# An encoder trunk on one core: gate products of the first 256 columns between transposes, the gate's bias added by TensorE, low parts on GpSimd

## The chip, the cores and the metric

The kernel runs on one core of a Trainium2 chip. The metric is the device time of one execution in microseconds. The engines are called by the profile's names: PE (TensorE, with PEld for its weight loads), DVE (VectorE), ACT (ScalarE), POOL (GpSimd) and SP (SyncE, which here only issues DMAs). Each executes its own list of instructions in order and waits on semaphores where it needs another's result.

## The reference

Two encoder layers over 1024 tokens of 1024 features, all in float32. The change concerns what follows the mixer in each layer:

```python
x = layer_norm(DEEPNORM_ALPHA * x + mix @ w_o[i], ln1_g[i], ln1_b[i])
ffn = expert_choice_moe(x, router_w[i], w1[i], w3[i], w2[i])
ple = jax.nn.sigmoid(x @ ple_gate_w[i] + ple_gate_b[i]) * (p[i] @ ple_w[i])
x = layer_norm(DEEPNORM_ALPHA * x + ffn + ple, ln2_g[i], ln2_b[i])
```

The router is a softmax of `x @ router_w` over 16 experts; each expert takes the 128 tokens with the highest affinity. `p` has 256 features per token. "PLE" below is the third line, and its gate is the sigmoid's argument.

## The kernel before, in words

**Precision.** PE multiplies in a reduced form of float32. A float32 operand is therefore split into a high part, which ACT makes by a cast (L82), and a low part, source minus high, made by DVE or POOL (L83). `mm3` (L87 to L89) forms a product by three matmuls: high by high, high by low, low by high.

**The tokens.** They stand in eight tiles of 128. `tail` multiplies the mixer's output by w_o tile by tile (PSUM tiles named S, two buffers) and `residual` makes the layer norm; its result x1 goes to DRAM (`keep_x1`, L1129 and L1132) and stays in SBUF. The last tile's norm is woven into the stage after it.

**The stage of the transposes** (`route`, from `residual(T - 1)`). `turn(t)` transposes tile t of x1 on PE (L157, eight transposes into two PSUM buffers of four) and splits the result: tiles 0 to 3 into xp, 4 to 7 into xk. `p_tile(i)` does the same for a tile of p (L1178, two transposes). The PSUM buffers named ps rotate among four, so that a transpose waits until DVE has taken the low part out of the buffer used four before. The order on PE is: turns 0 to 4, p tiles 0 to 3, the gate's bias by feature (L1215, for the experts' part), turns 5 to 7, p tiles 4 to 7. The order of all engines but SP is the order in which the code is written; SP's is set by a scheduler.

**The router.** Products with rws for 256, 256 and 512 tokens, each copied out by ACT (L1237); eight small transposes (L1241), then a softmax on DVE and ACT (L1244 to L1249, with the exponential on ACT). `back()` (L1258) turns the affinities for the choice of tokens. Between the router's copies ACT already casts PLE weights.

**The PLE's steps.** Tokens 0 to 511 are done here, the other half among the experts. There are sixteen steps: four groups n of 256 columns by four token tiles t. A step has 24 products of the gate (8 feature chunks by three matmuls) into pg and 6 of p @ ple_w into pw, both halves of one ps buffer. DVE adds the bias row (L1339), ACT takes the sigmoid (L1331) and copies pw (L1332, one buffer wv), POOL multiplies (L1333) and after two tiles issues a DMA that adds the result to acc in DRAM (L1335). `Feed` splits the weights ahead: of each ten, POOL takes six low parts and DVE four; sixteen split tiles (wk) rotate. Into the steps are woven: `back()` in step 0, sixteen rounds of top-k on DVE (L1267 to L1270), `merged` and `chosen` in the last steps. Raw weights lie in two rings; the first four gate chunks of 1 MB come through `ring_slot`.

**The experts** follow: about 1200 us of both layers together with PE multiplying, while 1 MB loads run ahead.

Of the kernel before, what the change touches and what calls it, by code (L numbers as in the profile page):

```python
# [20 lines left out]
D = 1024  # L21
S = 1024
T = 8
KC = 8
EPS = 1e-6
ALPHA = 4.0 ** 0.25
NEXP = 16
# [3 lines left out]
class Feed:  # L31
# [34 lines left out]
    def get(self, i):  # L66
        self.upto(i)
        return self.tiles[i]
# [6 lines left out]
class Body:  # L75
# [1071 lines left out]
    def route(self, L, x1, pl, residual, b, ctx_x):  # L1147

        nc, tc, h = self.nc, self.tc, self.h
        acc_d = self.acc_d[L]  # L1150
        TP = 4
        SP, SK = TP * 128, S - TP * 128
# [15 lines left out]
        rw = a.tile([128, KC, NEXP], F32, name="rw")  # L1168
        nc.sync.dma_start(rw, h["router_w"][L].rearrange("(k p) e -> p k e", p=128))
# [16 lines left out]
        for n in range(D // CW):  # L1186
            chunks.append(([128, KC, CW], [(lambda t: t, wg[:, :, n * CW:(n + 1) * CW])],
                           [lambda t, k=k: t[:, k, :] for k in range(KC)]))
            order += [(n, k) for k in range(KC)] + [(D // CW, 2 * n + k) for k in range(2)]
        chunks.append(([128, 2, D], [(lambda t: t, wp)],  # L1190
                       [lambda t, n=n, k=k: t[:, k, n * CW:(n + 1) * CW] for n in range(D // CW) for k in range(2)]))
        ring2 = lambda shape: raw2.tile(shape, F32, name="raw2", tag="raw2", bufs=5)
        feed = Feed(self, None, chunks, CW, WB, lo=[nc.gpsimd] * 6 + [nc.vector] * 4,
                    rings=[self.ring_slot] * 4 + [ring2], order=order)
        for k in range(4):
            feed.load(k)
# [1 line left out]
        def turn(t):  # L1198
            dst, u = (xp, t) if t < TP else (xk, t - TP)
            self.transpose_split(x1[t], dst[0], dst[1], u)  # L1200

        stats, scale, bias = residual(T - 1)
        turn(0)
        self.weave(stats[:2])
        turn(1)
        self.weave(stats[2:])
        turn(2)
        self.weave(scale)
        turn(3)
        turn(4)  # L1210
        self.weave(bias)
        for i in range(4):
            p_tile(i)
        pb = self.ps((128, KC))
        nc.tensor.transpose(pb, br, self.ident[:KC, :KC])  # L1215
        nc.vector.tensor_copy(bf, pb)
        self.split(rw, rws[:, 0], rws[:, 1])
        turn(5)
        turn(6)
        turn(7)  # L1220
        for i in range(4, T):
            p_tile(i)
        self.dump(f"x1_{L}", self.x1_d[L])
        ctx_x.close()
# [5 lines left out]
        brows = [c.tile([128, CW], F32, name="brow", bufs=2)]  # L1230
# [44 lines left out]

        def merged():

            tf = a.tile([48, 128], F32, name="tf")
            bt = a.tile([16, 2, 128], F32, name="bt")
            mt = a.tile([16, 3, 128], F32, name="mt")  # L1280
# [18 lines left out]
            self.dump(f"idx_{L}", idx)  # L1299

        step = 0
        for n in range(D // CW):
            cs = slice(n * CW, (n + 1) * CW)
            brow = brows.pop() if brows else c.tile([128, CW], F32, name="brow", bufs=2)
            self.row_bcast(brow, h["ple_gate_b"][L][cs])
            for t in range(TP):
                sl = slice(t * 128, (t + 1) * 128)
                if t % 2 == 0:
                    sgp = out2.tile([128, 2, CW], F32, name="sgT", bufs=2)
                sg = sgp[:, t % 2, :]  # L1310
                wv = out2.tile([128, CW], F32, name="wv", bufs=1)
                pgw = self.ps()
                pg, pw = pgw[:, :CW], pgw[:, CW:2 * CW]
                for k in range(10):
                    if t == 0:
                        feed.upto(10 * n + min(k + 1, 9))
                    w = feed.get(10 * n + k)
                    if k < KC:
                        self.mm3(pg, xp[0][:, k, sl], xp[1][:, k, sl], w[:, 0, :], w[:, 1, :], k == 0, k == KC - 1)
                    else:  # L1320
                        self.mm3(pw, pp[:, 0, k - KC, sl], pp[:, 1, k - KC, sl], w[:, 0, :], w[:, 1, :],
                                 k == KC, k == 9)
                    if t == TP - 1:
                        feed.upto(10 * n + min(k, 3) + WB)
# [5 lines left out]
                def finish(sg=sg, wv=wv, pw=pw, t=t, cs=cs, sgp=sgp):  # L1330
                    nc.scalar.activation(sg, sg, AF.Sigmoid)  # L1331
                    nc.scalar.copy(wv, pw)  # L1332
                    nc.gpsimd.tensor_mul(sg, sg, wv)  # L1333
                    if t % 2 == 1:
                        nc.gpsimd.dma_start(acc_d[(t - 1) * 128:(t + 1) * 128, cs].rearrange("(t p) c -> p t c", p=128), sgp,  # L1335
                                            accum_op=OP.add)

                step += 1
                nc.vector.tensor_add(sg, pg, brow)  # L1339
                if step == TP * D // CW:  # L1340
                    break
                if t == 0:
                    feed.upto(10 * n + WB - 1)
                for r in range(16 * (step - 1) // 13, min(16, 16 * step // 13)):
# [57 lines left out]
    def experts(self, L, gates, idx, idxf, count, moe, xk, pk, bf, SP, SK, out2, last):  # L1402
        nc, tc, h = self.nc, self.tc, self.h
        x1_d, acc_d = self.x1_d[L], self.acc_d[L]
        with ExitStack() as ctx:
# [89 lines left out]
            def ple(f):  # L1495

                pg, pw = self.ps(), self.ps()
                for k in range(10):
                    j = at[("ple", f, 0), k // 5]
                    feed.upto(j + LA)  # L1500
                    w = feed.get(j)
                    c = slice((k % 5) * 128, (k % 5) * 128 + 128)
                    if k < KC:
                        self.mm3(pg[:, :SK], w[:, 0, c], w[:, 1, c], xk[0][:, k, :], xk[1][:, k, :], k == 0, k == KC - 1)
                    else:
                        self.mm3(pw[:, :SK], w[:, 0, c], w[:, 1, c], pk[:, 0, k - KC, :], pk[:, 1, k - KC, :],
                                 k == KC, k == 9)
                    feed.drop(j)
                sg = out2.tile([128, SK], F32, name="sgT", bufs=2)
                nc.scalar.activation(sg, pg[:, :SK], AF.Sigmoid, bias=bf[:, f:f + 1])  # L1510
                nc.vector.tensor_mul(sg, sg, pw[:, :SK])

                def out():
                    p = self.ps((128, SK // 128, 128))
                    for t in range(SK // 128):
                        nc.tensor.transpose(p[:, t, :], sg[:, t * 128:(t + 1) * 128], self.ident)
                    ev = out2.tile([128, SK], F32, name="ev", bufs=2).rearrange("p (t c) -> p t c", c=128)
# [414 lines left out]
```

## Time and profile before

| | us |
|---|---|
| median of three runs | 2713.09 (2711.2 to 2713.68) |
| profiled execution, its own time | 2715.39 |
| its span, first to last instruction | 2713.7 |
| PE busy in the span | 2607.9 (96%) |
| DVE, ACT, POOL busy | 2192.4, 1769.1, 780.9 |
| mean granted TensorE clock | 0.982 of full |

A row of the timeline gives the start, the time until the last of the merged instructions ended, engine, line, operation and the number of instructions; in brackets stands the idle time before it and who ended it. A window's row gives each engine's busy time, the granted clock as a share of 2.4 GHz (0.50 is 1.2 GHz) and what the DMA engines did. The two layers go through the stage alike: layer 0 from 624.5 us on, layer 1 from 1967.2 us on.

### The profile page before, as it was taken

What the parts mean: (1) busy time and instruction counts of PE and PEld (TensorE: products, weight loads), DVE (VectorE), ACT (ScalarE), POOL (GpSimd) and SP (SyncE); (2) the same over time, 40 slices, a digit from 0 to 9 for tenths busy, and PEclk for the clock granted to TensorE, in tenths of its full rate; (3) what the DMA queues carried; (4) which work ended last, traced back from release to release, by engine and by line L of the source; (5) the groups of instructions that cost most, each with busy time, mean ns of one, the idle gap of its engine ahead of it and who ended that gap; (6) DMA issues with size and microseconds to landing.
All of it is one profiled execution on the core that took longest, in us unless ns stands there. A gap on an engine that the chain in (4) does not pass through costs nothing.

```text
span 2713.7 us, 37590 instructions
## 1 busy us (share of the span) xinstructions
PE 2607.9 (96%) x13446; PEld 2166.0 (80%) x13446; DVE 2192.4 (81%) x3084; ACT 1769.1 (65%) x2655; POOL 780.9 (29%) x682
## 2 busy tenths in 40 slices
PE   8996899998999999999899999999989999999996
PEld 7886688787988888888677788887878888888884
DVE  3448787765888888988888989997668888888897
ACT  3335688714577777877542799997056777777783
POOL 0023456302401101110363577663143101110104
PEclk9997999999999999999899999999999999999998
DMA  4215200364799999999620010004658999999994
GB/s 171 78 57 151 68 9 11 115 229 151 229 344 367 364 377 385 363 365 370 235 108 16 36 28 13 13 13 117 221 154 271 356 371 365 364 374 369 384 363 162
DMA packets 223178, 579.11 MB, mean 213 GB/s; under 512 B 19360, under 2 KB 87088, under 8 KB 222992
## 3 DMA queue, kind: packets, MB, share of 16 engines
q1 hardware_dynamic: 201264, 535.82, 53.0%
q0 software_dynamic: 21728, 40.90, 7.1%
q8 instruction: 106, 1.74, 0.3%
q14 instruction: 80, 0.66, 0.1%
HBM read 511.52 MB, written 63.96 MB: 212 GB/s over the span
## 4 chain that ended last, share of the span: by engine, by line
PE 84%; DVE 7%; ACT 4%; issue 2%; DMA 1%; POOL 1%; DVEq 0%; POOLq 0%; ACTq 0%; SPq 0%
PE S L87 11%; PE S L89 11%; PE S L88 11%; PE ps L87 9%; PE ps L89 8%; PE ps L88 8%; PE S L660 6%; PE ps L698 6%; PE ps L723 5%; PE ps L157 3%; PE ps L1689 2%; ACT pt L82 1%; PE ps L1691 1%; ACT p L667 1%; DVE st L556 1%
## 5 line engine op out<-in xcount | busy, mean ns | idle before, releaser
L83 DVE TENSOR_TENSOR wm<-raw,wm 128x1024 fp32r<-128x1024 f32 (+1 forms) x798 | 905.1, 1206 | 23.3 <-ACT wm L82 13.7
L82 ACT CAST wm<-raw 128x1024 fp32r<-128x1024 f32 (+1 forms) x800 | 783.2, 1046 | 80.5 <-PE S L89 76.1
L87 PE MATMUL S<-wm,xs 128*128 128x512 f32 x1024 | 401.3, 392 | 0.5 <-ACT xs L82 0.5
L89 PE MATMUL S<-wm,xs 128*128 128x512 f32 x1024 | 398.8, 389 | 0.0
L88 PE MATMUL S<-wm,xs 128*128 128x512 f32 x1024 | 398.5, 389 | 0.0
L689 POOL TENSOR_SCALAR p<-p,mx 128x1024 f32<-128x1024 f32 x190 | 214.5, 1129 | 188.4 <-DVE mx L688 181.1
L663 DVE TENSOR_REDUCE mx<-S 128x1 f32<-128x1024 f32 x192 | 234.3, 1221 | 38.1 <-PE S L660 32.9
L83 DVE TENSOR_TENSOR pt<-ps,pt 128x512 fp32r<-128x512 f32 x384 | 245.2, 680 | 23.6 <-ACT pt L82 22.5
L1492 POOL DMA_INDIRECT acc_d<-y,idx x30 | 48.4, 1615 | 748.6 <-ACT y L1491 648.6
L82 ACT CAST pt<-ps 128x512 fp32r<-128x512 f32 x384 | 206.2, 588 | 35.9 <-PE ps L723 34.7
L89 PEld LDWEIGHTS S<-wm,xs 128*128 128x128 f32 x1024 | 192.2, 188 | 41.0 <-DVE xs L83 0.9
L87 PEld LDWEIGHTS S<-wm,xs 128*128 128x128 f32 x1024 | 192.3, 188 | 39.7 <-ACT xs L82 1.0
L88 PEld LDWEIGHTS S<-wm,xs 128*128 128x128 f32 x1024 | 192.3, 188 | 38.7
L667 ACT ACTIVATE p<-S,mx 128x1024 f32<-128x1024 f32 x190 | 214.0, 1126 | 11.4 <-DVE mx L663 10.6
L723 PE MATMUL ps<-ident,p 128*128 128x128 f32 x1520 | 202.5, 274 | 7.2 <-DVE pt L83 4.6
L723 PEld LDWEIGHTS ps<-ident,p 128*128 128x128 f32 x1520 | 177.8, 141 | 38.1 <-DVE pt L83 6.6
L87 PE MATMUL ps<-wm,hh 128*128 128x512 f32 x480 | 189.6, 395 | 0.0
L89 PE MATMUL ps<-wm,hh 128*128 128x512 f32 x480 | 187.2, 390 | 0.0
L88 PE MATMUL ps<-wm,hh 128*128 128x512 f32 x480 | 186.9, 389 | 0.0
L698 PE MATMUL ps<-pt,vhl 128*128 128x512 f32 x512 | 149.6, 414 | 0.0
L1519 POOL DMA_DIRECT2D acc_d<-ev x16 | 22.3, 1397 | 320.0 <-ACT ev L1518 280.7
L940 ACT ACTIVATE mv<-mv 128x1 f32<-128x1 f32 x32 | 6.5, 203 | 160.1 <-DVE mv L939 160.1
(454 smaller groups left out, 5467.7 us busy)
## 6 DMA issues: line engine op xcount, KB each, us to landing
raw<-in_w_dram SPq DMA_DIRECT2D x384, 1024.0 KB
raw<-in_w_o_dram SPq DMA_DIRECT2D x8, 1024.0 KB
raw<-in_ple_gate_w_dram SPq DMA_DIRECT2D x8, 1024.0 KB
x_d<-x SPq DMA_DIRECT2D x16, 512.0 KB
acc_d<-r SPq DMA_DIRECT2D x16, 512.0 KB
raw<-in_ple_gate_w_dram SPq DMA_DIRECT2D x16, 512.0 KB
r<-acc_d SPq DMA_DIRECT2D x16, 512.0 KB
raw<-in_w_in_even_dram SPq DMA_DIRECT2D x6, 1024.0 KB
```

The costliest lines, as they stand in the source:

```text
L82: self.nc.scalar.copy(hi, src)
L83: (eng or self.nc.vector).tensor_sub(lo, src, hi.bitcast(F32))
L87: mm(out, lh, rh, start=start, stop=False)
L88: mm(out, lh, rl, start=False, stop=False)
L89: mm(out, ll, rh, start=False, stop=stop)
L157: nc.tensor.transpose(p[:, k, :], src[:, (4 * j + k) * 128:(4 * j + k + 1) * 128], self.ident)
L660: nc.tensor.matmul(s[:, n * 512:(n + 1) * 512], u["q"][j][:, u["qt"] * 128:(u["qt"] + 1) * 128], u["k"][j][:, n * 512:(n + 1) * 512], star ...
L663: nc.vector.tensor_reduce(mx[:, 0:1], s, axis=AX.X, op=OP.max, negate=True)
L667: self.nc.scalar.activation(p, u["s"], AF.Exp, bias=mx[:, 0:1], accum_out=mx[:, 1:2])
L689: nc.gpsimd.tensor_scalar(P[i], P[i], mx[:, 2:3], 1.0, op0=OP.mult, op1=OP.mult)
L698: nc.tensor.matmul(po[g], v(4 * half + m), pt[half][z][:, m, :], start=half + m + z == 0, stop=half == 1 and m == 3 and z == 1)
L723: nc.tensor.transpose(pp[:, m, :], p[:, kt * 128:(kt + 1) * 128], self.ident)
```

## The change

Of the gate, the first group of columns (n = 0) for the four tiles t leaves the steps: `early_gate(t)` computes it into an S buffer between the later turns, and ACT puts its sigmoid in sg0. Its eight weight tiles are split in pairs by `early_weights(i)`, with the low parts on POOL, the first pair into wa, the others into the buffers of x1's tiles 0 to 2, which are then no longer needed. In every gate the bias is added by two matmuls: `pick`, a constant that selects row n of four, times the high and low parts of the bias rows, `bros`; the DVE addition goes. All four p tiles of the middle move behind turn 7. The low parts of all PLE weights go to POOL. Top-k rounds are set out by a new table, in which steps 0 to 2 and 4 have none; rw moves to a pool of its own, and two tiles of `merged` and one of the experts' move to other memory.

```diff
-        feed = Feed(self, None, chunks, CW, WB, lo=[nc.gpsimd] * 6 + [nc.vector] * 4,
+        feed = Feed(self, None, chunks, CW, WB, lo=nc.gpsimd,
                     rings=[self.ring_slot] * 4 + [ring2], order=order)
...
+        for n in range(NB):
+            nc.gpsimd.tensor_copy(pick[:, n, :], self.ident[:NB, n:n + 1].to_broadcast([NB, 128]))
...
+        brow = e.tile([NB, CW], F32, name="brow")
+        nc.sync.dma_start(brow, h["ple_gate_b"][L].rearrange("(n c) -> n c", c=CW))
...
+        def early_weights(i):
+            w = wa if i == 0 else b.tile([128, 2, 2, CW], F32R, name=f"x1_{i - 1}")
+            for j in range(2):
+                k = 2 * i + j
+                w0[k] = w[:, j]
+                self.split(feed.raw[0][:, k, :], w[:, j, 0, :], w[:, j, 1, :], nc.gpsimd)
...
+        def gate(pg, t, w, n):
+            sl = slice(t * 128, (t + 1) * 128)
+            for z in range(2):
+                nc.tensor.matmul(pg, pick[:, n, :], bros[:, z, :], start=z == 0, stop=False)
+            for k in range(KC):
+                wk = w(k)
+                self.mm3(pg, xp[0][:, k, sl], xp[1][:, k, sl], wk[:, 0, :], wk[:, 1, :], False, k == KC - 1)
...
+        def early_gate(t):
+            if t % 2 == 0:
+                pgs.append(self.ps2())
+            pg = pgs[-1][:, (t % 2) * 512:(t % 2) * 512 + CW]
+            gate(pg, t, w0.get, 0)
+            nc.scalar.activation(sg0[:, t, :], pg, AF.Sigmoid)
...
         stats, scale, bias = residual(T - 1)
+        self.split(brow, bros[:, 0, :], bros[:, 1, :], nc.gpsimd)
+        early_weights(0)
         turn(0)
         self.weave(stats[:2])
         turn(1)
         self.weave(stats[2:])
+        early_weights(1)
         turn(2)
         self.weave(scale)
+        early_weights(2)
         turn(3)
+        early_weights(3)
         turn(4)
         self.weave(bias)
-        for i in range(4):
-            p_tile(i)
+        early_gate(0)
...
+        turn(5)
+        early_gate(1)
         self.split(rw, rws[:, 0], rws[:, 1])
-        turn(5)
         turn(6)
+        early_gate(2)
         turn(7)
-        for i in range(4, T):
+        early_gate(3)
+        for i in range(T):
             p_tile(i)
...
+        ROUNDS = [0, 0, 0, 1, 1] + [1 + 15 * i // 9 for i in range(1, 10)] + [16] * 3
...
+                if n:
+                    gate(pg, t, get, n)
...
-                    nc.scalar.activation(sg, sg, AF.Sigmoid)
+                    if n:
+                        nc.scalar.activation(sg, pg, AF.Sigmoid)
                     nc.scalar.copy(wv, pw)
-                    nc.gpsimd.tensor_mul(sg, sg, wv)
+                    nc.gpsimd.tensor_mul(sg, sg if n else sg0[:, t, :], wv)
...
-                nc.vector.tensor_add(sg, pg, brow)
```

What the change does to ACT's list at the head of the stage in layer 0 (a difference, + is new; mv is the last tile's norm, L945 its scaling, x_0 to x_2 the reused buffers with weights):

```order
 L940 ACTIVATE mv<-mv 128x1
+L82 CAST bros<-brow 4x256
+L82 CAST wa<-raw 128x256 x2
 L82 CAST xp_5464<-ps 128x4x128 x4
 L940 ACTIVATE mv<-mv 128x1
+L82 CAST x_0_5537<-raw 128x256 x2
 L82 CAST xp_5464<-ps 128x4x128 x2
 L945 ACTIVATE x_7_4805<-r,mv 128x512 x2
+L82 CAST x_1_5563<-raw 128x256 x2
 L82 CAST xp_5464<-ps 128x4x128 x2
+L82 CAST x_2_5582<-raw 128x256 x2
 L82 CAST xk_5450<-ps 128x4x128 x2
```

The casts of the bias rows and of the weights stand ahead of those of the turned tiles.

SP's queue at the same place (the new load of w is one of the experts' chunks, into the ring slot of the first gate chunk):

```order
 L1166 DMA br<-in_ple_gate_b_dram 8x128
-L1169 DMA rw<-in_router_w_dram 128x8x16
+L1212 DMA rw<-in_router_w_dram 128x8x16
+L1215 DMA brow<-in_ple_gate_b_dram 4x256
+L47 DMA raw<-in_w_dram 128x2x1024
 L1129 DMA x_d_76<-x_7_4805 128x1024
 L1132 DMA acc_d_78<-r 128x1024
```

The bias rows, brow, are asked for third, and a 1 MB load has moved ahead of the last tile's stores.

PE's list behind the router in layer 0, as it is now (lg and af are the router's scores and affinities, pp is p turned):

```order
L1288 MATMUL ps<-ident,lg 128x16 x8
L87 MATMUL ps<-wk,pp 128x256
L88 MATMUL ps<-wk,pp 128x256
L89 MATMUL ps<-wk,pp 128x256
L87 MATMUL ps<-wk,pp 128x256
L88 MATMUL ps<-wk,pp 128x256
L89 MATMUL ps<-wk,pp 128x256
L1305 MATMUL ps<-ident,af 16x128 x8
```

Before, 24 products with xp stood between the first row and the second; they are in the transposes' stage now.

## Rows read from the trace of the kernel before

**Rows 1.** The page, the chain that ended last: shares of the span by engine.

```profile
PE 84%; DVE 7%; ACT 4%; issue 2%; DMA 1%; POOL 1%; DVEq 0%; POOLq 0%; ACTq 0%; SPq 0%
```

**Rows 2.** Windows of layer 0: the transposes, the PLE's steps, the experts.

```profile
core 0: us, PE busy (x) PEld busy (x) DVE busy (x) ACT busy (x) POOL busy (x), PEclk, DMA share, GB/s
624.50:646.35 21.85, 14.92 (x83) 11.41 (x81) 16.95 (x36) 12.72 (x27) 3.55 (x3) 0.77 0.34 108
...
658.50:715.00 56.50, 56.50 (x481) 56.17 (x481) 48.02 (x123) 25.08 (x69) 33.24 (x42) 1.00 0.52 131
...
740.00:800.00 60.00, 60.00 (x283) 49.77 (x282) 51.82 (x50) 45.10 (x52) 5.84 (x4) 1.00 0.95 334
```

**Rows 3.** The timeline of PE in the transposes of layer 0.

```profile
624.49 1.91 PE L157 MATMUL ps<-ident,x 128*128 128x128 f32 x16
...
635.65 2.48 PE L1178 MATMUL ps<-ident,pl 128*128 128x128 f32 x8 [2.99 <-DVE xp L83]
...
639.31 5.30 PE L157 MATMUL ps<-ident,x 128*128 128x128 f32 x24
...
646.35 0.29 PE L87 MATMUL ps<-xp,rws 128*16 128x256 f32 x1
```

**Rows 4.** The timeline of ACT in the same stretch.

```profile
625.12 2.06 ACT L82 CAST xp<-ps 128x512 fp32r<-128x512 f32 x4 [8.04 <-PE ps L157]
...
632.89 1.52 ACT L945 ACTIVATE x<-r,mv 128x512 f32<-128x512 f32 x2 [1.77 <-DVE mv L969]
634.31 1.05 ACT L82 CAST xp<-ps 128x512 fp32r<-128x512 f32 x2
```

**Rows 5.** The timeline of SP's queue in the same stretch.

```profile
624.68 0.34 SPq L1166 DMA_DIRECT2D br<-in_ple_gate_b_dram  x1
625.12 0.40 SPq L1169 DMA_DIRECT2D rw<-in_router_w_dram  x1
```

**Rows 6.** Windows of half a microsecond behind the issue of rw.

```profile
626.00:626.50 0.50, 0.40 (x4) 0.16 (x2) 0.50 (x2) 0.50 (x2) 0.00 (x0) 1.00 0.41 47
626.50:627.00 0.50, 0.37 (x3) 0.37 (x4) 0.50 (x2) 0.50 (x2) 0.00 (x0) 1.00 0.87 84
627.00:627.50 0.50, 0.50 (x5) 0.32 (x4) 0.50 (x2) 0.18 (x1) 0.00 (x0) 1.00 0.00 0
```

**Rows 7.** Timelines of SP, ACT and PE in the transposes of layer 1.

```profile
1964.72 0.43 SPq L1169 DMA_DIRECT2D rw<-in_router_w_dram  x1
...
1967.79 2.05 ACT L82 CAST xp<-ps 128x512 fp32r<-128x512 f32 x4 [8.04 <-PE ps L157]
...
1976.97 1.05 ACT L82 CAST xp<-ps 128x512 fp32r<-128x512 f32 x2
...
1988.58 0.29 PE L87 MATMUL ps<-xp,rws 128*16 128x256 f32 x1
```

**Rows 8.** Timelines of DVE, ACT and POOL around the router of layer 0.

```profile
645.88 1.44 DVE L83 TENSOR_TENSOR pk<-ps,pk 128x256 fp32r<-128x256 f32 x4
...
649.56 1.32 ACT L82 CAST wk<-raw 128x256 fp32r<-128x256 f32 x4
...
650.04 4.41 POOL L83 TENSOR_TENSOR wk<-raw,wk 128x256 fp32r<-128x256 f32 x6 [10.31 <-ACT wk L82]
```

**Rows 9.** Timelines of ACT and DVE behind the router of layer 0.

```profile
660.38 0.31 ACT L1246 ACTIVATE af<-af 128x128 f32<-128x128 f32 x1
...
661.28 0.29 DVE L1249 TENSOR_TENSOR af<-af,sm 128x128 f32<-128x128 f32 x1
...
662.91 1.18 ACT L1259 COPY aff<-ps 16x512 f32<-16x512 f32 x2 [2.21 <-PE ps L1258]
```

**Rows 10.** The timeline of POOL in the PLE's steps of layer 0.

```profile
676.85 1.21 POOL L1335 DMA_DIRECT2D acc_d<-sgT  x1 [0.31 <-POOL sgT L1333]
677.65 4.63 POOL L83 TENSOR_TENSOR wk<-raw,wk 128x256 fp32r<-128x256 f32 x6
```

**Rows 11.** Windows of the transposes of layer 0, cut where the granted clock changes.

```profile
626.00:634.00 8.00, 4.16 (x28) 2.67 (x26) 5.87 (x15) 3.46 (x8) 0.22 (x1) 1.00 0.08 9
634.00:644.50 10.50, 7.93 (x34) 6.52 (x35) 8.05 (x17) 6.95 (x15) 3.33 (x3) 0.51 0.49 167
```

**Rows 12.** Groups of instructions in the PLE's steps of layer 0.

```profile
L1333 POOL TENSOR_TENSOR sgT<-sgT,wv 128x256 f32<-128x256 f32 x14 | 11.6, 832 | 14.7 <-ACT wv L1332 14.7
L1267 DVE MAX8 top<-aff 48x8 f32<-48x512 f32 x16 | 10.9, 679 | 1.4 <-ACT aff L1259 1.3
```

More of the change, by code (lines that the diff above doesn't have):

```diff
@@ L1167, in route @@
         xp = [a.tile([128, KC, SP], F32R, name=f"xp{i}") for i in range(2)]
-        rw = a.tile([128, KC, NEXP], F32, name="rw")
-        nc.sync.dma_start(rw, h["router_w"][L].rearrange("(k p) e -> p k e", p=128))
+        ctx_e = ExitStack()
         rws = a.tile([128, 2, KC, NEXP], F32R, name="rws")
@@ L1188, in route @@
                            [lambda t, k=k: t[:, k, :] for k in range(KC)]))
-            order += [(n, k) for k in range(KC)] + [(D // CW, 2 * n + k) for k in range(2)]
+            order += ([(n, k) for k in range(KC)] if n else []) + [(D // CW, 2 * n + k) for k in range(2)]
         chunks.append(([128, 2, D], [(lambda t: t, wp)],
@@ L1200, in turn @@
             self.transpose_split(x1[t], dst[0], dst[1], u)
+        w0 = {}
+        sg0 = a.tile([128, TP, CW], F32, name="sg0")
+        NB = D // CW
+        pick = a.tile([NB, NB, 128], F32R, name="pick")
+        for n in range(NB):
+            nc.gpsimd.tensor_copy(pick[:, n, :], self.ident[:NB, n:n + 1].to_broadcast([NB, 128]))
+        bros = a.tile([NB, 2, CW], F32R, name="bros")
+        e = ctx_e.enter_context(self.pool("early", "right"))
+        rw = e.tile([128, KC, NEXP], F32, name="rw")
+        nc.sync.dma_start(rw, h["router_w"][L].rearrange("(k p) e -> p k e", p=128))
+        wa = e.tile([128, 2, 2, CW], F32R, name="wa")
+        brow = e.tile([NB, CW], F32, name="brow")
[13 more added lines that the diff above has]
+                self.mm3(pg, xp[0][:, k, sl], xp[1][:, k, sl], wk[:, 0, :], wk[:, 1, :], False, k == KC - 1)
+        pgs = []
+        def early_gate(t):
[4 more added lines that the diff above has]
+            nc.scalar.activation(sg0[:, t, :], pg, AF.Sigmoid)
         stats, scale, bias = residual(T - 1)
+        self.split(brow, bros[:, 0, :], bros[:, 1, :], nc.gpsimd)
+        early_weights(0)
         turn(0)
@@ L1216, in route @@
         nc.vector.tensor_copy(bf, pb)
+        turn(5)
+        early_gate(1)
         self.split(rw, rws[:, 0], rws[:, 1])
-        turn(5)
         turn(6)
+        early_gate(2)
         turn(7)
-        for i in range(4, T):
+        early_gate(3)
+        for i in range(T):
             p_tile(i)
         self.dump(f"x1_{L}", self.x1_d[L])
+        ctx_e.close()
         ctx_x.close()
@@ L1229, in route @@
         c = feed.pool = ctx_2.enter_context(self.pool("ple2"))
-        brows = [c.tile([128, CW], F32, name="brow", bufs=2)]
         for xs, s0, o, n in ((xp, 0, 0, SP // 2), (xp, SP // 2, SP // 2, SP // 2), (xk, 0, SP, SK)):
@@ L1276, in merged @@
         def merged():
-            tf = a.tile([48, 128], F32, name="tf")
-            bt = a.tile([16, 2, 128], F32, name="bt")
-            mt = a.tile([16, 3, 128], F32, name="mt")
+            tm = a.tile([48, 8, 128], F32, name="tm", tag="lg", bufs=1)
+            tf, bt, mt = tm[:, 0, :], tm[0:16, 1:3, :], tm[0:16, 3:6, :]
             nc.vector.tensor_copy(tf, ti)
@@ L1301, in route @@
         step = 0
+        ROUNDS = [0, 0, 0, 1, 1] + [1 + 15 * i // 9 for i in range(1, 10)] + [16] * 3
         for n in range(D // CW):
             cs = slice(n * CW, (n + 1) * CW)
-            brow = brows.pop() if brows else c.tile([128, CW], F32, name="brow", bufs=2)
-            self.row_bcast(brow, h["ple_gate_b"][L][cs])
+            i0 = 10 * n - KC
             for t in range(TP):
@@ L1313, in route, with get @@
                 pg, pw = pgw[:, :CW], pgw[:, CW:2 * CW]
-                for k in range(10):
+                def get(k):
                     if t == 0:
[L1316 to L1322, printed above, removed]
-                    if t == TP - 1:
-                        feed.upto(10 * n + min(k, 3) + WB)
+                        feed.upto(i0 + min(k + 1, 9))
+                    w = feed.get(i0 + k)
+                    if t == TP - 1:
+                        feed.upto(i0 + min(k, 3) + WB)
+                    return w
+                if n:
+                    gate(pg, t, get, n)
+                for k in range(KC, 10):
+                    w = get(k)
+                    self.mm3(pw, pp[:, 0, k - KC, sl], pp[:, 1, k - KC, sl], w[:, 0, :], w[:, 1, :],
+                             k == KC, k == 9)
                 if step == 0:
@@ L1328, in route, with finish @@
                     moe[0].load(len(moe[0].raw))
-                def finish(sg=sg, wv=wv, pw=pw, t=t, cs=cs, sgp=sgp):
-                    nc.scalar.activation(sg, sg, AF.Sigmoid)
+                def finish(sg=sg, wv=wv, pg=pg, pw=pw, t=t, cs=cs, sgp=sgp, n=n):
+                    if n:
+                        nc.scalar.activation(sg, pg, AF.Sigmoid)
                     nc.scalar.copy(wv, pw)
-                    nc.gpsimd.tensor_mul(sg, sg, wv)
+                    nc.gpsimd.tensor_mul(sg, sg if n else sg0[:, t, :], wv)
                     if t % 2 == 1:
@@ L1342, in route @@
                 if t == 0:
-                    feed.upto(10 * n + WB - 1)
-                for r in range(16 * (step - 1) // 13, min(16, 16 * step // 13)):
+                    feed.upto(i0 + WB - 1)
+                for r in range(ROUNDS[step - 1], ROUNDS[step]):
                     top_round(r)
@@ L1516, in out @@
                         nc.tensor.transpose(p[:, t, :], sg[:, t * 128:(t + 1) * 128], self.ident)
-                    ev = out2.tile([128, SK], F32, name="ev", bufs=2).rearrange("p (t c) -> p t c", c=128)
+                    ev = a.tile([128, SK], F32, name="ev", bufs=2).rearrange("p (t c) -> p t c", c=128)
                     nc.scalar.copy(ev, p)
```

## The prediction

> **What bounds the kernel now.** I read the page's chain first: TensorE (PE) carries 84% of it [rows 1]. So a change pays where PE stands idle, and costs wherever PE gets more to do. Then I read the windows by stage [rows 2]: the PLE steps and the experts keep PE busy from end to end, the transposes of x1 don't: 21.85 us with 14.92 us of PE, part of that at a granted clock below 1. That stage, once per layer, is what the change works on. PE's own timeline [rows 3] shows the largest hole: after the fifth tile PE waits 2.99 us for VectorE (DVE). The holes are due to a chain over the other engines: ScalarE (ACT) rounds each transposed tile, DVE takes the low part, and both also run the last tile's layer norm. ACT's rows [rows 4] show it: the fourth tile is rounded at 634.31 only after the two scaling ops of the norm.
>
> **The change part by part.** Durations are those of the profiled execution (2715.39 us, span 2713.7; the median of the runs is 2713.09, 2.3 lower). I work out how much later the router's products begin, then how much shorter the steps get.
>
> *1. The wait at the front.* ACT gets three casts (the bias rows, two weights) ahead of its first tile. The bias rows come by a DMA that stands third on SP's queue, behind br, which leaves at 624.68 when PE ends the output projection, and rw at 625.12 [rows 5]; so it leaves at about 625.56. In the quiet queue rw's packets ran from 626.0 to 627.0 [rows 6]. The bias rows lie behind them: no landing before 627.0. I take 627.4, with 0.4 us for four rows and the signal (chosen; bounds: no wait at all, or 628.5). A weight cast takes 0.33 us (1.32 for four) [rows 8], and I take the bias rows' cast at as much. With 3 x 0.33 the first tile is rounded at 628.4 instead of 625.12: **+3.25 us** in layer 0. Everything on DVE but the residual add is queued behind that in program order, so nothing catches up. In layer 1 rw is issued at 1964.72, 3.1 us ahead of the first rounding; with the same 1.85 us from issue to landing, and 0.5 for gate weights still on their way (chosen), the bias rows are there at 1967.5 and the first tile is rounded at 1968.5 instead of 1967.79 [rows 7]: **+0.7 us**.
>
> *2. The rest up to the first gate.* Two weight casts now stand ahead of the third tile, for which DVE already waits, and two ahead of the fourth: 4 x 0.33 = 1.3 us. The fourth tile of layer 0 is rounded at 634.31 + 3.25 + 1.3 = 638.9, its two casts take 1.0 and the last two weights 0.65. GpSimd (POOL) makes the low parts at 0.735 us each (4.41 for six [rows 8]), the first from 640.25 on: done at 641.7. The first gate's last three products need them: it ends at 642.1. Its 26 products had room from about 637 on, so they are hidden; its end isn't, it is set by ACT and POOL.
>
> *3. From there PE is the bound.* Turn 5, 6, 7 are 24 transposes at 0.113 us (16 take 1.91 with 0.2 for the tail of the last, at full clock [rows 3]), with br's 2.8 us. Three gates are 3 x 26 products of 256 columns at 0.1175 (56.50 us for 481 instructions [rows 2]): 9.2 us. A gate's bias product also waits for the previous sigmoid where both write one PSUM tile; it is ready under the transposes between. Then all eight p tiles, four of which stood in the hole before: the last needs the buffer of the fourth, behind sigmoid (0.4), a cast (0.31) and four DVE ops of 0.36 (1.44 [rows 8]), 2.7 us in all. The router begins at 642.1 + 2.8 + 9.2 + 2.7 = 656.8 instead of 646.35 [rows 3]: **+10.4**. The same from the fourth tile of layer 1, 1976.97 [rows 7]: 1976.97 + 0.7 + 1.3 + 17.9 = 1996.9 instead of 1988.58: **+8.3**. Together +18.7 us. PE's added work there is 104 products, 12.2 us per layer; so only 2 and 4 us of them vanish in the holes.
>
> *4. The steps.* Out go 96 products (-11.3 us per layer), in come two bias products for each of the other 12 steps, 24 x 0.1175 = +2.8. Two covers are lost. Step 0 had 30 products (3.5 us) under which the router's softmax ran; now it has 6 (0.7 us, to 659.3 in the old times). The softmax can't be quicker: ACT makes three weight casts, loads the exponential's table, runs it from 660.38 to 660.69, and DVE ends at 661.57 [rows 9]. PE waits **+2.3** before it can turn the affinities back. Step 2 then needs step 0's PSUM buffer, which ACT frees behind two copies of 1.18 us together [rows 9]: +0.7. The two PLE weights of step 4 are last on POOL, behind three multiplications (0.83 in the mean [rows 12]) and an accumulating DMA (1.21 after a gap of 0.31 [rows 10]): +0.8, counted from the buffers' order. Sum -11.3 + 2.8 + 2.3 + 0.7 + 0.8 = **-4.7 per layer**, -9.4 in both.
>
> *5. Costed at nothing.* DVE loses its bias additions and 16 low parts per layer; PE didn't wait for either. The sixteen top-k rounds now run without a break, about 2.3 us each (three ops like the top's 0.68 [rows 12], two short loads, gaps): 36 us from about 663.5, so until 700 in the old times of the steps, some 3 us before PE asks. On POOL a group of four steps needs 10 low parts x 0.77 (4.63 for six beside a busy DVE [rows 10]) + 4 x 0.83 + 2 x 1.5 = 14.0 us against 32 x 4 x 0.1175 = 15.0 of PE, so POOL stays hidden by 1.0 us. On SP a 1 MB load for the experts goes ahead of tile 7's stores and the PLE weights: the weights land some 3 us later against PE, which has got 10 us later itself. The experts' loads start later with the router; PE was at 60.00 of 60.00 us there [rows 2], and the reserve of chunks is the same.
>
> Sum: 18.7 - 9.4 = +9.3 us; 2713.1 + 9.3 = **2722.4 us**, 0.34% slower.
>
> **The clock.** In layer 0 the granted clock averages 0.51 from 634.0 to 644.5, nearly all of it its lower level (1.2 GHz), after a stretch in which PE was busy for 4.16 of 8.00 us, and it is back at 1.00 (2.4 GHz) once PE has been busy nearly without a break from 639.3; the 24 transposes took 5.30 us there [rows 3, 11]. In the changed order the first gate makes PE busy from 637 on, ahead of my PE-bound tail, so I count the tail at full clock. If instead the first 5 us of it run at half, each layer pays 2.5 us more; that is the upper bound.
> The Trainium skill, "TensorE: Matmul & The Clock Gate" (Part 1), has the reduced clock as the default and activity as what releases it: by that rule the gates keep the clock up, and the trace agrees in that the clock came back during the dense transposes. With the rule the sum stays +9.3, without it it would be +14.
>
> **The rivals.**
> *A, faster: the holes take the gates.* If PE found the weights and tiles in time, the 12.2 us would go into idle time and the router begin hardly later. For it: 21.85 us minus 81 transposes at 0.113 leaves 12.7 us of holes at full clock, just enough. Against it: most of them lie before ACT has rounded the fourth tile, and the gates but the first stand behind that. With no growth the result is 2 x -4.7 = -9.4: 2704 us. It decides in favour of the change where the stage grows by less than 4.7 us per layer; I get 10.4 and 8.3.
> *B, no change: the bias rows are in time.* If the DMA lands before PE ends the projection, the three casts lie in ACT's idle time and 3.25 + 0.7 fall away: +5.3, 2718.4 us, at the edge of what can be told. Against it: br's release by PE at 624.68 in layer 0.
> *C, slower still: POOL becomes the bound of the steps.* If a low part took half more than it did, 1.15 us, a group would need 17.8 us instead of 15.0, and 2.8 us x 3 groups x 2 layers adds 17: 2739 us; it decides from 0.87 us per low part. Against it: six took 4.41 with DVE quiet and 4.63 with DVE busy [rows 8, 10].
> The Trainium skill, "GPSIMD Engine Reference" (1. Specifications), says that GpSimd shares its SBUF interfaces with VectorE and meets contention where VectorE has two SBUF inputs. The trace shows 5% of it.
>
> **How the numbers follow.** About 0.2%, 5.4 us, can be told from no change. The forecast has 0.62, A 0.08, B 0.17, C or a half clock in the tail 0.13. B lies on the edge: with the forecast's own lower end, same gets 0.22; faster is A, 0.08; slower 0.70. The forecast's bounds: without the two small stalls -3, without the front wait -4 (2715); with half a clock +5, a landing 1 us later +1 (2728). I widen below toward A and above toward C: 2711 to 2731.
>
> **What would show it.** Right: the first rounding of layer 0 some 3 us after PE's first transposes, with ACT waiting for the bias rows; the router about 32 us after the projection's end (was 21.9); PE idle for some 2 us ahead of the affinities' transposes; no PE wait in the later steps. Wrong: a router that begins less than 5 us later, top-k or POOL releasing PE in the steps, or a half clock through the last gates.

## The result and the profile after

The changed kernel takes 2739.18 us (median of four runs, 2736.16 to 2741.2) against 2713.39 for the kernel before: 1.0095 times as long (95% interval 1.0078 to 1.0113), 25.8 us slower. The forecast was 2722.4 us, with 2711 to 2731 as its range: the direction was right, the size was not.

The page's line of busy times answers to the table of the kernel before:

```profile
PE 2629.9 (96%) x13510; PEld 2177.7 (80%) x13510; DVE 2173.0 (79%) x3020; ACT 1770.2 (65%) x2659; POOL 806.4 (29%) x724
```

PE is busy for 22.0 us more than before, though it executes only 64 matmuls more (13510 instead of 13446): the 32 bias pairs. In the profiled execution (span 2736.1 us) I cut each layer at four places that both kernels have: the first transposes of x1, the router's first product, the transposes of the affinities, the first product of the experts' part (`xk,wm`), and the first product of expert 0 (`wm,xs`).

| stretch, layer 0 / layer 1 | before, us | after, us | change | forecast |
|---|---|---|---|---|
| stage of the transposes | 21.86 / 21.43 | 31.85 / 31.47 | +9.99 / +10.04 | +10.4 / +8.3 |
| router to affinities | 15.86 / 15.86 | 15.28 / 15.28 | -0.58 | -0.5 |
| affinities to the experts' part | 54.10 / 54.10 | 56.47 / 56.34 | +2.37 / +2.24 | -4.2 |
| its first product to expert 0 | 8.31 / 8.31 | 9.76 / 9.86 | +1.45 / +1.55 | 0 |
| sum | 100.13 / 99.70 | 113.36 / 112.95 | +13.2 / +13.3 | +5.7 / +3.6 |

The two layers give 26.5 us. (The forecast's -4.7 per layer stands here as -0.5 and -4.2. The profiled execution reached layer 0's stage 4.0 us earlier than that of before, so its span grew only by 22.4; the medians show 25.8.) Both stages come out near their forecasts. The miss is in the lower rows: +6.5 and +1.5 us per layer.

**The stage.** PE's timeline of the stage in layer 0 (start, time to the last end, engine, line, operation, count; in brackets the idle time before and its releaser) answers to [rows 3]:

```profile
620.47 1.91 PE L157 MATMUL ps<-ident,x 128*128 128x128 f32 x16
623.45 1.26 PE L157 MATMUL ps<-ident,x 128*128 128x128 f32 x8 [1.07 <-DVE xp L83]
625.83 1.97 PE L157 MATMUL ps<-ident,x 128*128 128x128 f32 x8 [1.13 <-DVE xp L83]
628.77 1.97 PE L157 MATMUL ps<-ident,x 128*128 128x128 f32 x8 [0.97 <-DVE xp L83]
630.67 0.79 PE L1228 MATMUL S<-bros,pick 4*128 4x256 f32 x2
...
636.34 0.22 PE L1259 MATMUL ps<-ident,br 8*128 8x8 f32 x1
636.49 1.09 PE L157 MATMUL ps<-ident,x 128*128 128x128 f32 x8
637.51 0.50 PE L1228 MATMUL S<-bros,pick 4*128 4x256 f32 x2
...
640.90 1.04 PE L157 MATMUL ps<-ident,x 128*128 128x128 f32 x8
...
650.97 1.43 PE L1177 MATMUL ps<-ident,pl 128*128 128x128 f32 x8 [0.32 <-DVE pp L83]
```

The first gate ends 15.9 us after the first transposes (forecast 17.6), and from there PE is the bound, as forecast: each turn with its gate takes 4.4 us (636.49 to 640.90). Most of the front wait is missing. ACT and SP show why (same columns):

```profile
621.17 0.41 ACT L82 CAST bros<-brow 4x256 fp32r<-4x256 f32 x1 [8.11 <-PE ps L157]
...
622.10 2.00 ACT L82 CAST xp<-ps 128x512 fp32r<-128x512 f32 x4
```
```profile
617.69 0.35 SPq L1166 DMA_DIRECT2D br<-in_ple_gate_b_dram  x1
...
618.55 0.67 SPq L1215 DMA_DIRECT2D brow<-in_ple_gate_b_dram  x1
```

br no longer waits for PE's end, as it did before [rows 5]; presumably its place is free earlier in the new layout of memory, though no row shows addresses. (In the run below that has neither pick nor bros, br leaves in layer 0 at PE's end again, 0.19 us after the first transposes.) The bias rows' DMA leaves 1.9 us ahead of the first transposes. What is left of the wait are the three casts: ACT begins the first of them 0.70 us after the first transposes, and the first tile is rounded 1.63 us after them instead of 0.63 [rows 4].

**The steps.** PE at the affinities, and two windows after them (start:end, length, busy us of PE, PEld, DVE, ACT, POOL with counts, granted clock, DMA share, GB/s):

```profile
665.21 0.28 PE L89 MATMUL ps<-wk,pp 128*128 128x256 f32 x1
667.60 1.87 PE L1305 MATMUL ps<-ident,af 128*16 128x128 f32 x8 [2.11 <-DVE af L1296]
669.12 0.56 PE L87 MATMUL ps<-wk,pp 128*128 128x256 f32 x1
669.48 0.41 PE L88 MATMUL ps<-wk,pp 128*128 128x256 f32 x1
...
673.24 0.50 PE L1228 MATMUL ps<-bros,pick 4*128 4x256 f32 x2
```
```profile
668.00:670.00 2.00, 2.00 (x11) 1.59 (x10) 0.00 (x0) 1.07 (x2) 0.00 (x0) 0.50 0.77 305
670.00:672.00 2.00, 2.00 (x11) 2.00 (x11) 1.75 (x5) 0.83 (x3) 0.96 (x2) 0.50 0.45 182
```

The wait for the softmax is there with the forecast size (2.11 us). Behind it stands something not forecast: the granted clock is 0.50 (1.2 GHz), and 8 transposes with 18 products take 5.64 us (667.60 to 673.24); at the full-clock rates of the prediction they take about 3.1. So 2.5 us are lost there. (The same 26 instructions took 3.11 us in a run below in which the clock stayed up.)

Later every step takes 4.15 us instead of 3.52, with PE never idle. The seam between two steps shows where:

```profile
693.81 0.28 PE L89 MATMUL ps<-wk,pp 128*128 128x256 f32 x1
694.02 0.50 PE L1228 MATMUL ps<-bros,pick 4*128 4x256 f32 x2
694.45 0.38 PE L87 MATMUL ps<-wk,xp 128*128 128x256 f32 x1
694.67 0.28 PE L88 MATMUL ps<-wk,xp 128*128 128x256 f32 x1
```

Products follow each other every 0.12 us; around the bias pair the starts are 0.21, 0.43 and 0.22 apart. The pair adds 0.63 us to the step, not 2 x 0.1175. The weight loads (PEld, the loads of the stationary operands) of the pair and of the product behind it begin only with their own products, at 694.01 and 694.45:

```profile
694.01 0.29 PEld L1228 LDWEIGHTS ps<-bros,pick 4*128 4x128 f32 x2
694.45 0.19 PEld L87 LDWEIGHTS ps<-wk,xp 128*128 128x128 f32 x1
```

And the experts' part begins with two PE waits that did not exist before:

```profile
724.07 0.50 PE L87 MATMUL ps<-xk,wm 128*128 128x512 f32 x1 [0.81 <-ACT wm L82]
...
725.70 0.50 PE L89 MATMUL ps<-xk,wm 128*128 128x512 f32 x1 [0.90 <-POOL wm L83]
```

### The profile page after: what moved, and what is told of

The parts are those of the page before. It is cut to its first block, busy times and chain, and to the rows that moved or that the text cites. A ratio compares the mean times of both kernels' runs of the same rounds, so it can differ in the third digit from the quotient of the medians.

```text
span 2736.1 us, 37631 instructions
## 1 busy us (share of the span) xinstructions
PE 2629.9 (96%) x13510; PEld 2177.7 (80%) x13510; DVE 2173.0 (79%) x3020; ACT 1770.2 (65%) x2659; POOL 806.4 (29%) x724
```

## The experiments

### What the bias pair costs

Theory 1: the pair is dear because its stationary operand has fewer than 128 rows. First run:

```diff
-        pick = a.tile([NB, NB, 128], F32R, name="pick")
+        pick = a.tile([128, NB, 128], F32R, name="pick")
...
-        brow = e.tile([NB, CW], F32, name="brow")
+        brow = e.tile([128, CW], F32, name="brow")
+        nc.gpsimd.memset(brow, 0.0)
```

> The changed kernel, with pick and the bias rows on 128 partitions instead of 4 (rows 4 to 127 of the bias rows are zero), so that a bias matmul has a stationary operand of 128 rows as every gate product has. Theory 1 (a bias pair costs 0.63 us instead of 0.235 because its stationary operand has only 4 rows): a pair falls to 0.24 us, a step from 4.15 to 3.76 us, 32 pairs in two layers give 32 x 0.4 = 12.6 us: about 2726.5. Rival 1 (it is the break in the chain of products, or two products of one stationary operand, whatever its rows): the pair stays at 0.6 and the time at 2739. Rival 2 (POOL bounds the steps): 2739 too, with PE waiting where it now works.

Measured: 2732.89 us. A step falls to 3.77 us, as theory 1 has it, but the stage grew to 32.3 and 32.5 us. My clearing stood on POOL behind pick's casts, which wait for PE, so the bias rows' DMA left late and ACT waited for it:

```profile
624.37 0.26 SPq L1216 DMA_DIRECT2D brow<-in_ple_gate_b_dram  x1
```
```profile
625.85 0.40 ACT L82 CAST bros<-brow 128x256 fp32r<-128x256 f32 x1 [10.47 <-DMA brow<-in_ple_gate_b_dram]
```

Here was the forecast's front wait, by accident. The next run clears ahead of pick:

```diff
+        brow0 = e.tile([128, CW], F32, name="brow")
+        nc.gpsimd.memset(brow0, 0.0)
         pick = a.tile([128, NB, 128], F32R, name="pick")
```

> As the run with 128 rows, but the rows are cleared on POOL ahead of pick's casts, so that the bias rows' DMA is issued before PE ends the projection (in that run it was issued 3 to 4 us later than in the changed kernel, and ACT waited for it with the first tile: the front wait of the prediction, brought back by accident). Theory 1: the first tile is rounded about 1.5 us after PE's first transposes instead of 4.0, the stage shrinks by 1.6 us per layer against the changed kernel (four pairs), the steps as in that run: 2739 - 12.6 = about 2726.5. Rival: the stage does not depend on this wait because DVE bounds it: 2732 as there.

Measured: 2727.41 us, as expected; the stage takes 29.92 and 29.90 us. Between these two runs the first tile of layer 0 is rounded 3.98 and 1.56 us after the first transposes, and the stage differs by the same 2.42 (layer 1: 2.56 and 2.56): with the early gates behind it, a wait at the front goes into the stage in full. The seam in this run, with the next product after 0.12, 0.23 and 0.12 us:

```profile
692.66 0.28 PE L89 MATMUL ps<-wk,pp 128*128 128x256 f32 x1
692.78 0.40 PE L1230 MATMUL ps<-bros,pick 128*128 128x256 f32 x2
693.01 0.28 PE L87 MATMUL ps<-wk,xp 128*128 128x256 f32 x1
693.13 0.28 PE L88 MATMUL ps<-wk,xp 128*128 128x256 f32 x1
```

Its weight loads begin with the product ahead of the one that needs them, as those of the other products do:

```profile
692.66 0.31 PEld L1230 LDWEIGHTS ps<-bros,pick 128*128 128x128 f32 x2
692.90 0.19 PEld L87 LDWEIGHTS ps<-wk,xp 128*128 128x128 f32 x1
```

Is it the number of rows? The same kernel with 64 instead of 128 in pick, bros and brow0:

> The run with 128 rows, clearing first, but on 64 partitions: does the pair's price follow the number of rows of the stationary operand? If any row count short of 128 breaks PE's overlap, a step takes 4.15 us as with 4 rows and the time is about 2739; if it goes by the rows, a step lies between 3.77 and 4.15; if only very few rows are dear, 3.77 and 2727.

Measured: 2738.92 us (two runs), a step of 4.15 us again:

```profile
694.92 0.28 PE L89 MATMUL ps<-wk,pp 128*128 128x256 f32 x1
695.13 0.50 PE L1230 MATMUL ps<-bros,pick 64*128 64x256 f32 x2
695.56 0.39 PE L87 MATMUL ps<-wk,xp 128*128 128x256 f32 x1
695.78 0.29 PE L88 MATMUL ps<-wk,xp 128*128 128x256 f32 x1
```

4 and 64 rows cost the same, 128 rows cost nothing beyond the products. So the price is that of leaving the full row count and coming back: at both changes the next weights are not loaded under the product that still runs. (The moving operand, the bias rows, changes its row count along with pick; no run separates the two.)

### The bias by DVE, as before

```diff
-            for z in range(2):
-                nc.tensor.matmul(pg, pick[:, n, :], bros[:, z, :], start=z == 0, stop=False)
...
+                if n:
+                    nc.vector.tensor_add(sg, pg, brow)
```

(and the same addition behind each early gate)

> The changed kernel with the bias added by DVE, as before, in the steps and after the early gates; no bias matmul, no pick. Theory 1: 32 pairs at 0.63 us go, 20 us, and nothing comes in their place because DVE has time: about 2719, a step at 3.53 us. Rival 1 says the same of the pairs. Rival 2 (POOL bounds the steps, or the steps are long for another reason): a step shrinks by less than half of that, and the time stays above 2729. If the front wait of the prediction counted, the three casts are now two and the stage loses another 0.3 us.

Measured: 2736.9 us (2736.55 to 2742.36), only 2.3 below the changed kernel and within the spread of the two; the expected 2719 was a miss. The steps are at 3.52 to 3.56 us, but PE has three new waits:

```profile
641.99 0.39 PE L87 MATMUL S<-wa,xp 128*128 128x256 f32 x1 [2.26 <-DVE sg L1233]
707.63 0.39 PE L88 MATMUL ps<-wk,xp 128*128 128x256 f32 x1 [0.80 <-POOL wk L83]
718.99 0.23 PE L1333 MATMUL ps<-ident,tm 16*128 16x16 f32 x1 [1.35 <-DVE tm L1327]
```

Two early gates share a PSUM tile, so the second waits for DVE's addition; low parts come late; and with DVE at the additions too the top-k is late. The addition on PE does relieve DVE, which I had costed at nothing.

### The low parts shared again

```diff
-        feed = Feed(self, None, chunks, CW, WB, lo=nc.gpsimd,
+        feed = Feed(self, None, chunks, CW, WB, lo=[nc.gpsimd] * 6 + [nc.vector] * 4,
```

> The changed kernel with the low parts of the PLE weights shared again, six on POOL and four on DVE of each ten. Theory 1 (PE alone bounds the steps): no change, 2737 to 2741, since PE is busy 4.00 of 4.00 us in the steps. Rival 2 (POOL with all low parts bounds the steps): a step shrinks by 0.3 us or more, 10 us in all: 2729 or less. A third way: DVE's low parts delay the top-k, and PE waits for it at the end of the steps: 2742 or more.

Measured: 2743.18 us (2736.32 to 2743.71), 1.0098 times the kernel before: no gain over the changed kernel. The steps stay at 4.15 us, and PE waits 0.24 and 0.57 us for the top-k at their end, as the third way has it. Rival C, POOL as the bound of the steps, is out.

### Without the early gates

The kernel before with the bias by 4-row products, the low parts on POOL and `merged`'s tiles where the change has them:

```diff
-                for k in range(10):
+                for z in range(2):
+                    nc.tensor.matmul(pg, pick[:, n, :], bros[:, z, :], start=z == 0, stop=False)
+                for k in range(10):
```

> The kernel before with two of the three parts: the bias by matmuls with 4 rows, all low parts on POOL. The early gates are out: 96 products are back in the steps, p tiles and router where they stood. Theory 1: the kernel before plus 32 pairs at 0.63 us: 2713.4 + 20 = 2733.5; so the early gates by themselves cost about 6 us net (their 22.6 us out of the steps do not pay for a stage some 9 us longer per layer plus the wait and the half clock around the affinities). Rival 3 (the early gates alone are the loss and a pair costs 0.235): 2713.4 + 7.5 = 2721.

Measured: 2734.55 us, with 22.00 and 22.44 us for the stage and steps of 4.15. The kernel before took 2713.92 beside it, so 20.6 of the 25.8 us are there without any early gate. The same kernel with 128 rows:

> The run without early gates, with pick and bias rows on 128 partitions. Theory 1: 32 pairs at 0.25 instead of 0.63 us: 2734.5 - 12.2 = about 2722, that is the kernel before plus 8 us for the bias products alone; no front wait, since no tile stands behind the bias rows there. Rival: the pair's price depends on its surroundings, or the low parts on POOL cost something by themselves: 2726 or more.

Measured: 2725.44 us: 9.1 less, where 12.2 were expected. The steps fall to 3.77 us; the stage grew by 1.3 and 0.2 us. I had written that there would be no front wait, and there was one: the bias rows' DMA left in layer 0 at 623.79, 0.6 us after PE's first transposes, and ACT's casts of the tiles stand behind the cast of the bias rows here too. Against the run with 4 rows the first tile is rounded 1.95 and 0.37 us later; without early gates the stage takes only a part of that.

### back() later

```diff
-        ROUNDS = [0, 0, 0, 1, 1] + [1 + 15 * i // 9 for i in range(1, 10)] + [16] * 3
+        ROUNDS = [0, 0, 0, 0, 0] + [1 + 15 * i // 9 for i in range(1, 10)] + [16] * 3
...
-                if step == 0:
+                if step == 4:
                     back()
```

(The rounds of step s are those from entry s to entry s + 1 of the table. In the changed kernel steps 0, 1 and 3 have none; "steps 0 to 2 and 4" ahead of the prediction was wrong.)

> The changed kernel with back() moved from step 0 to step 4, and the top-k rounds begun there (the table's first five entries are 0). Theory 5: PE no longer waits 2.1 us for the softmax, and since it stays busy, the granted clock does not fall to its lower level for the steps after (half clock for about 4 us, 2 us lost): 4 us per layer, 2731. Rival 5a: the fall of the clock has another cause (the short steps of six products, the 16-row transposes): only the wait goes, 2735. Rival 5b: the top-k now ends too late and PE waits for it near step 15: some of it comes back there, 2735 or more.

Measured: 2734.36 us, 4.8 less. By the time alone this is nearer to the rivals' 2735 than to 2731; the clock speaks for theory 5, for it stays up where it had fallen to 0.50, although four short steps of six products now follow each other:

```profile
668.00:670.00 2.00, 2.00 (x19) 1.86 (x17) 0.81 (x3) 1.34 (x3) 2.00 (x4) 1.00 0.00 0
670.00:672.00 2.00, 2.00 (x16) 1.86 (x16) 0.37 (x1) 0.90 (x3) 1.20 (x3) 1.00 0.85 266
```

But the wait does not always bring the fall. Eight of the kernels, the changed one among them, have the wait of 2.1 us in both layers. Around it the clock fell in 13 of these 16 places; it stayed up in three: in layer 1 of the first run with 128 rows, of the run with 64 rows and of the run with the ring that turned (below). In the six layers with back() later it never fell there. The run with 64 rows, layer 1:

```profile
2025.78 1.04 PE L1307 MATMUL ps<-ident,af 128*16 128x128 f32 x8 [2.11 <-DVE af L1298]
2028.89 0.50 PE L1230 MATMUL ps<-bros,pick 64*128 64x256 f32 x2
2033.25 0.39 PE L88 MATMUL ps<-wk,pp 128*128 128x256 f32 x1 [0.73 <-POOL wk L83]
```
```profile
2026.00:2028.00 2.00, 2.00 (x20) 1.90 (x18) 0.23 (x1) 1.46 (x3) 0.00 (x0) 1.00 0.73 270
```

The stretch from the affinities to the experts' part takes 55.35 us there, against 56.47 and 56.34 in the changed kernel with the same price of a pair. So the fall costs about 1 us net: where the clock stays up, the late weights behind it, with their wait of 0.73, take back part of the 2.5 us.

Part of the gain of this run comes back one step on: the last weights of step 4, whose lateness the forecast priced at 0.8 us, now show; behind the affinities' wait they had been hidden.

```profile
674.74 0.38 PE L88 MATMUL ps<-wk,pp 128*128 128x256 f32 x1 [1.12 <-POOL wk L83]
```

### The waits where the experts begin

In the changed kernel ACT's first cast for the experts waits for the last product of the steps:

```profile
723.29 1.35 ACT L82 CAST wm<-raw 128x640 fp32r<-128x640 f32 x2 [3.64 <-PE ps L89]
```

Theory 4: its tile lies over the buffers of the last four split weights; with 32 weights instead of 40 through 16 buffers, others stand last in them. (In three layers, one each of the first run with 128 rows, the run with 64 rows and the run with the bias by DVE, the clock also fell around PE's two waits here, and the stretch to expert 0 took 11.1 us instead of 9.8.) To turn the ring by eight I first took eight tiles without using them:

```diff
         c = feed.pool = ctx_2.enter_context(self.pool("ple2"))
+        for _ in range(8):
+            c.tile([128, 2, CW], F32R, name="wk", tag="wk", bufs=WB)
```

> The changed kernel with one edit: eight tiles of the ring of split weights (wk) are handed out unused ahead of the first, so that the last two weights of the steps lie in the buffers that they had in the kernel before (38 and 39 of 40, there 6 and 7 modulo 16, now 30 and 31). Theory 4: the experts' first two weight casts on ACT wait for the very last products of the steps only because the new memory of the experts lies over the last two of 32 weights; with the shift they start a step earlier, PE no longer idles 0.81 and 0.90 us there, and each layer gains 1.4 to 2.8 us: 2733.5 to 2736. Rival: the casts are late because the raw weights or the order on ACT are late: no change, 2739, PE's two waits stay.

Measured: 2737.75 us, the waits unchanged: by itself a miss for theory 4. But as I read it, tiles that are never written take no buffers, so that all weights lay where they had lain; no row shows addresses. With a memset of eight elements per partition on each tile they do:

> The run with eight unused tiles of the weight ring, mended: there the unused tiles took no buffers, so that the weights and the experts' first tile lay exactly where they lie in the changed kernel, and the edit was none. Here each of the eight is written (8 elements per partition on POOL), so it takes its buffer, and the experts' first split weight lies over buffers that the last four weights no longer use. Theory 4 as before: that weight's cast no longer waits for the very last products of the steps, PE's waits of 0.81 and 0.90 us go, and the stretch from the last top-k transposes to the experts' hundredth product shrinks from 31.2 to about 28.8 us (it is 28.4 in the kernel before): 4 to 5 us in both layers, about 2734.5. Rival: the second cast, which waits for the last gate product as in the kernel before, keeps PE waiting just as long: 2738 or more.

Measured: 2734.89 us, as expected. ACT and PE:

```profile
721.75 0.73 ACT L82 CAST wm<-raw 128x640 fp32r<-128x640 f32 x1
724.68 0.73 ACT L82 CAST wm<-raw 128x640 fp32r<-128x640 f32 x1 [2.20 <-PE ps L89]
```
```profile
725.07 0.28 PE L89 MATMUL ps<-wk,pp 128*128 128x256 f32 x1
725.19 0.39 PE L87 MATMUL ps<-xk,wm 128*128 128x512 f32 x1
```

The first cast begins 3.4 us ahead of the product that needs it, PE goes over without a gap, and the last stretch of the table is 8.30 us, as before the change. The edit turns the ring and adds eight small memsets, nothing else, so theory 4 holds.

### Together

Three edits at once (128 rows, the ring without effect, back() in step 4):

> The three edits together (128 rows with the clearing first, the ring shifted by eight, back() in step 4). If the three causes are independent, their gains add up: 12.6 + 4 + 8 = 25 us, so about 2714.5, the time of the kernel before, and what the early gates put into the stage (about 9 us per layer) is then just what they save in the steps. If they overlap (a later wait takes the place of one that is removed), 2720 or more.

Measured: 2727.07 us instead of 2714.5, no better than 128 rows alone: the gains overlap. back() in step 4 had its gain taken by the low parts (1.50 us) and by the top-k:

```profile
713.95 0.23 PE L1344 MATMUL ps<-ident,tm 16*128 16x16 f32 x1 [1.12 <-DVE tm L1338]
```

With the effective ring, and back() in step 3 (`ROUNDS = [0, 0, 0, 0, 1] + ...`):

> 128 rows with the clearing first, the mended ring, and back() in step 3 instead of 0: the most that I can take out of the changed kernel's losses at once. In step 4 the move of back() had met two new waits, 1.1 to 1.5 us for POOL's low parts of that step's last weights and 1.1 us for the top-k at the end; in step 3 PE waits about 0.5 us for the softmax, and the top-k starts 5 us earlier. Theory: per layer 29.9 us for the stage, about 21 to the first steps' end, and in all 117.5 to 118 us from the stage's start to the experts' hundredth product, against 116.4 in the kernel before: 2713.7 + 3 = 2716 to 2717. Rival: the waits only move again (POOL or top-k): 2722 or more, as in the run with three edits (2727) less the ring's 4 to 5.

Measured: 2716.61 us (2712.97 to 2718.23), 1.0009 times the kernel before (1.0000 to 1.0018), as expected. From stage to expert 0 a layer takes 101.4 us against 100.13 and 99.70. The wait at the affinities is down to this:

```profile
664.56 1.03 PE L1309 MATMUL ps<-ident,af 128*16 128x128 f32 x8 [0.44 <-DVE af L1300]
```

With the three edits all but 3 us of the loss is gone. No version beat the kernel before. An estimate of what is left: 32 pairs with 128 rows lengthen the way from the router to the experts' part by 4.06 us per layer in the run without early gates, 8.1 in both, so the rest of this last kernel gains some 5 us. Whether another way to add the bias would keep them is open: by DVE it brought waits of its own (2.26, 0.80 and 1.35 us in layer 0).

## Why the prediction was right in direction and wrong in size

*1 and 2, the front.* The mechanism was right (2.42 us of wait cost 2.42 us of stage), its condition was not met: I read the release of br off the trace of the kernel before, and in the new kernel br leaves 2.8 us ahead of the first transposes instead of 0.2 behind. This is rival B's condition, but the casts did not lie in idle time, as B has it: they still cost 1.0 and 0.9 us. B's 2718 was further off. The first gate's end, by ACT and POOL, was right: forecast 17.6 us with a wait of 3.25, measured 15.9 with 1.0.

*3, the PE-bound tail.* Right in kind; three pairs make it 1.2 us longer. At half clock (0.50 in layer 0 from 626 to 634) the first gate ends 15.9 us after the start, at full clock and with 128 rows 15.2, since it waits for ACT and POOL there anyway: clock and pair cost 0.8 us here. So +10.4 became +9.99 (front -2.2, pairs +1.2, clock), and +8.3 became +10.04 (front +0.2, and the same two).

*4, the steps: the step that failed.* "In come two bias products ... 24 x 0.1175 = +2.8": the pair costs 0.63 us instead of 0.235, so 12 pairs add 4.7 us per layer, and those of the early gates 1.6 more. The run with 128 rows, cleared first, took 11.8 us back. The wait of 2.3 for the softmax came as 2.11, but with it, in both layers of the changed kernel, 2.5 us of half clock: my clock paragraph looked at the stage's tail and not at the hole that the sum itself had made. The two small stalls, 0.7 and 0.8, stayed behind these, so that the half clock cost about 1 us net. With the 0.81 us of point 5: -4.2 + 4.7 + 2.5 - 1.5 + 0.8 = +2.3, as measured.

The Trainium skill, "TensorEngine Tiling (Array Packing)" (Key Properties), says that a change of tiling mode drains the TensorE; under "Available Configurations" it lists modes of 128, 64 and 32 rows. The trace agrees: 64 and 4 rows add 0.39 us per pair, 128 rows nothing, and it is at the two changes of the row count that the weights are not loaded ahead. That this is the drain of which the Trainium skill speaks is an inference; no row names a mode.

*5, costed at nothing.* POOL, DVE and the top-k did stay hidden in the changed kernel. What I missed is memory: fewer weights through the same ring moved the last ones under the experts' first tile, 0.81 and 0.90 us of PE wait, about 2.3 us per layer in all with what follows. (The ring's run gave 4.3 us for both layers.)

*Rivals and signs.* A fell: the stage grew by 10, not by less than 4.7. C gave the measured time, 2739, by the wrong mechanism: sharing the low parts again gained nothing. The 5% that I read there as contention is no more than spread: at 664.65 in the trace of the kernel before six low parts took 4.24 us, with DVE busy for 3.73 of them. Three of the four signs that I had named for being right came (the stage's length, PE's 2.1 us ahead of the affinities, no wait in the later steps) and none of those for being wrong: not one of them looked at the price of a pair.

## What to carry to other kernels

Before a product is priced at the rate of its neighbours, look at the row count of its stationary operand: here short ones between full ones cost two breaks, and padding them with zeros to 128 rows took the breaks away. Work taken out of a dense stretch uncovers what ran under it, and a hole in PE's work may cost more in clock, though not each time. Name signs for the cheap terms of a sum too. When an edit changes how many tiles pass through a ring, see which buffers the last ones hold and what is laid over them next; a DMA's release in the old trace need not hold in the new layout.

## What I had not expected of the hardware

A matmul with 4 or 64 rows between 128-row ones spreads the starts around it to 0.21, 0.43 and 0.22 us, where 128 rows give 0.12, 0.23 and 0.12; the weights behind a change of the row count are loaded only with their own product. The granted clock was 0.50 from 668 to 672 us behind a PE wait of 2.11 us. The same wait in 16 layers brought such a fall in 13 and none in three; with a wait of 0.44 us or none (twelve layers) the clock stayed at 1.00 there.
